# Moving the base inverse of the first two delta heads ahead of the third head's preparation

## The chip, the cores and the metric

The kernel runs on one core of one Trainium2 chip. The metric is the device time of one execution in microseconds (us). The core has five engines that matter here, each with its own queue of instructions, which it works through in order: TensorE (PE for the matmuls, PEld for its weight loads), VectorE (DVE), ScalarE (ACT), GpSimd (POOL), and SyncE (SP), which here issues all DMA transfers.

## The reference

The reference computes one layer of a bidirectional encoder trunk, on 1024 tokens of width 1024, in float32. The layer has three parts, each with a norm before and after it: a mixer, a cross-attention into 256 memory tokens, and a feed-forward network. The change lies in the mixer, which has two branches that start from one input projection: eight heads of windowed attention, and four heads of a gated delta rule, run in both directions. For each delta head, direction and chunk of tokens the delta rule needs the solution of a unit lower triangular system:

```python
lower = jnp.where(strict, jnp.einsum('bhnid,bhnjd->bhnij', kb, k) * decay, 0.0)
tmat = lower + jnp.eye(c, dtype=jnp.float32)
rhs = jnp.concatenate([v * beta[..., None], kb * jnp.exp(g)[..., None]], axis=-1)
sol = lax.linalg.triangular_solve(tmat, rhs, left_side=True, lower=True, unit_diagonal=True)
```

A scan over the chunks follows, which multiplies the solutions with a running state. The outputs of both branches go through one output projection.

## The kernel before

The kernel uses chunks of 128 tokens, eight of them (NT), and inverts each 128 x 128 triangular matrix explicitly, in two steps. The **base inverse** inverts its four 32 x 32 diagonal blocks; the **levels** then join these blocks to 64 x 64 and to 128 x 128 with small matmuls.

The work of the mixer is listed in three tables of short names, ORDER_1 to ORDER_3 (lines 36 to 38), which `issue` (line 700) walks through:

- **D h** (`delta_proj`, line 694) projects key, query and value of delta head h: for each of the three, `proj` (line 264) loads a 512 KB weight tile, splits it into a high and a low part (`split`, line 99: ACT casts, DVE subtracts) and runs 48 matmuls (line 261) into two PSUM banks of the pool `pg`, which has three. `conv` (line 276) then copies the banks with ACT (lines 283, 284) and runs the four other taps of the convolution on DVE (line 286).
- **P h** (`prep`, line 425) makes what the delta rule needs of head h: decays (`gm`, line 457, on DVE, into the matmul of line 458), transposes (line 438), products of keys (line 477) stored to `d_u` (line 480), and the scaled beta values (`beta2`, line 472).
- **B g** (`base_inverse`, line 503) is the base inverse of the pair g of heads (B0 for heads 0 and 1, B1 for heads 2 and 3), all 128 blocks of a pair at once, one in each partition. It transposes `beta2` on PE (line 508), copies it with ACT (line 510), sends it through DRAM (lines 511, 522, 523), loads the blocks from `d_u` into tile `V` (line 515), forms `A` on DVE (lines 525, 527), masks it on POOL (line 528), and then runs 30 rounds of two DVE instructions, each of which needs the one before (lines 534 and 536). Two scalings on DVE (lines 538, 539) and four stores to `d_inv` (line 543) end it. Tiles `V` and `A` exist once, so B1 cannot fill them until B0 has stored them.
- **L h** (`levels`, line 546) fetches the blocks of head h from `d_inv` in 20 small transfers (line 551) and `d_u` (line 572), and joins them: transposes (line 576), then two rounds of a matmul of line 585, a copy on ACT, a matmul of line 591, and copies on ACT and DVE. The result goes to `d_pz` (line 610).
- **G h** and **A ct**, **V** are the projections of the gate and of the attention's queries (A0 to A3), keys (A4) and values. They call the same `proj`. A rotates the result on DVE (lines 726, 727, 732) with four small transfers in between (line 731, tile `rot`), then stores it.
- **W** (`next_windows`, line 678) does two windows of the attention: scores (line 633), softmax, transposes (line 656), products with the values (line 661). Its tiles, among them `vhl` for the values, are in a pool that is opened after the pool of `V` and `A` is closed, so they may lie in the same memory.
- **s01** is a step of the scan of both pairs (`scan`, line 768, matmuls of line 782), **M**, **K**, **V** of ORDER_3 belong to the memory tokens.

```python
ORDER_1 = "D0 P0 D1 P1 D2 P2 D3 P3 B0 B1".split()
ORDER_2 = "L0 L1 G0 G1 A4 V A0 A1 L2 L3 W W W A2 A3 G2 G3 W".split()
ORDER_3 = ("M " + "s01 W K " * 5 + "s01 K " * 3 + "s01 V V").split()
```

The tables do not set the order of the instructions alone. The framework's scheduler (`schedule_with_timeline_sim=True`, line 1512) places every instruction on its engine's queue, by the order in which the code issues it, by what it depends on, and by its own model of durations; loads and splits of weights are raised by a fixed priority (line 120). So instructions of different names come to lie between each other. Once placed, each engine's order is fixed.

Of the kernel before, what the change touches and what calls it, by code (L numbers as in the profile page):

```python
# [32 lines left out]

ORDER_1 = "D0 P0 D1 P1 D2 P2 D3 P3 B0 B1".split()
ORDER_2 = "L0 L1 G0 G1 A4 V A0 A1 L2 L3 W W W A2 A3 G2 G3 W".split()
ORDER_3 = ("M " + "s01 W K " * 5 + "s01 K " * 3 + "s01 V V").split()

# [36 lines left out]
def tile_hybrid_block(  # L76
# [623 lines left out]
    def issue(order, table):  # L700
        for o in order:
            table[o[0]](*(int(c) for c in o[1:]))

    issue(ORDER_1, {"D": delta_proj, "P": lambda h: prep(h, *kqv[h]), "B": base_inverse})
    pp_.close()
# [811 lines left out]
```

## Time and profile before

| what | value |
|---|---|
| median of three runs | 1592.68 us (1585.84 to 1593.12) |
| profiled execution | 1592.72 us, of which 1591.0 us are the span from the first to the last instruction |
| mean granted TensorE clock | 0.976 of full speed |
| busy share of the span: PE, PEld, DVE, ACT, POOL | 96%, 80%, 67%, 44%, 20% |
| matmuls, DVE instructions | 7451, 1774 |
| HBM traffic | 153 GB/s over the span |

All times below are from the profiled execution, in us from the start of its span. How to read the views: "idle before" is the time in which the engine had nothing running just ahead of an instruction, with what ended it behind the arrow; in the table of stages each engine has its busy time and, in brackets, its instructions, then come the granted clock of TensorE (1.00 is full speed), the share of the DMA engines and GB/s; the timeline has the start, the duration, and the instruction. Matmuls are pipelined, so that durations of neighbours overlap: what a matmul takes of PE's time is read from one start to the next. SPq is the queue of SyncE, whose durations are those of issuing a transfer and not of the transfer. L534 is line 534.

### The profile page before, as it was taken

What the parts mean: (1) busy time and instruction counts of PE and PEld (TensorE: products, weight loads), DVE (VectorE), ACT (ScalarE), POOL (GpSimd) and SP (SyncE); (2) the same over time, 40 slices, a digit from 0 to 9 for tenths busy, and PEclk for the clock granted to TensorE, in tenths of its full rate; (3) what the DMA queues carried; (4) which work ended last, traced back from release to release, by engine and by line L of the source; (5) the groups of instructions that cost most, each with busy time, mean ns of one, the idle gap of its engine ahead of it and who ended that gap; (6) DMA issues with size and microseconds to landing.
All of it is one profiled execution on the core that took longest, in us unless ns stands there. A gap on an engine that the chain in (4) does not pass through costs nothing. (4 is left out here: it accounts for less than half of the span.)

```text
span 1591.0 us, 20951 instructions
## 1 busy us (share of the span) xinstructions
PE 1524.5 (96%) x7451; PEld 1270.5 (80%) x7451; DVE 1067.4 (67%) x1774; ACT 706.4 (44%) x1352; POOL 311.2 (20%) x305
## 2 busy tenths in 40 slices
PE   6999999789999998999999999999999999999998
PEld 5888888678899877788888777788888888888776
DVE  6777768766899974443346448776867654587565
ACT  6665551124655563564335565323222332344532
POOL 2000010000002300253302140433434333100021
PEclk9999999886999999999999999999999999999999
DMA  6244354684997484354223164443434333863354
GB/s 205 68 133 129 119 152 132 159 231 116 334 334 258 147 291 151 141 185 155 70 67 108 52 209 149 126 133 118 139 106 153 99 100 100 282 214 113 106 171 160
DMA packets 267366, 247.16 MB, mean 155 GB/s; under 512 B 39016, under 2 KB 204797, under 8 KB 267261
## 3 DMA queue, kind: packets, MB, share of 16 engines
q1 hardware_dynamic: 267261, 245.82, 48.9%
q8 instruction: 59, 0.97, 0.3%
q14 instruction: 46, 0.38, 0.1%
HBM read 173.65 MB, written 69.50 MB: 153 GB/s over the span
## 5 line engine op out<-in xcount | busy, mean ns | idle before, releaser
L102 ACT CAST whi<-wraw 128x1024 fp32r<-128x1024 f32 x108 | 113.2, 1049 | 186.9 <-PE pg L261 37.6
L103 DVE TENSOR_TENSOR wlo<-wraw,whi 128x1024 fp32r<-128x1024 f32 x78 | 95.9, 1231 | 90.5 <-ACT whi L102 86.3
L261 PE MATMUL pg<-hhi,whi 128*128 128x512 f32 x352 | 141.4, 403 | 9.9 <-DVE rop L727 9.9
L261 PE MATMUL pg<-hlo,whi 128*128 128x512 f32 x352 | 140.5, 400 | 0.0
L261 PE MATMUL pg<-hhi,wlo 128*128 128x512 f32 x352 | 139.8, 398 | 0.0
L1013 PE MATMUL pmg<-whi,b 128*128 128x512 f32 x384 | 119.8, 399 | 2.6 <-ACT whi L102 2.2
L1188 PE MATMUL pA<-s,whi 128*128 128x512 f32 x352 | 111.4, 397 | 1.2 <-ACT m L1205 1.2
L103 POOL TENSOR_TENSOR wlo<-wraw,whi 128x1024 fp32r<-128x1024 f32 x30 | 73.8, 2460 | 146.8 <-ACT whi L102 126.3
L261 PEld LDWEIGHTS pg<-hhi,whi 128*128 128x128 f32 x352 | 66.7, 190 | 25.6 <-DVE rop L727 10.0
L1013 PEld LDWEIGHTS pmg<-whi,b 128*128 128x128 f32 x384 | 72.2, 191 | 18.2 <-ACT whi L102 2.6
L261 PEld LDWEIGHTS pg<-hhi,wlo 128*128 128x128 f32 x352 | 66.6, 189 | 15.7
L261 PEld LDWEIGHTS pg<-hlo,whi 128*128 128x128 f32 x352 | 66.6, 189 | 15.2
L1188 PEld LDWEIGHTS pA<-s,whi 128*128 128x128 f32 x352 | 65.2, 187 | 16.8 <-ACT m L1205 1.9
L1378 PE MATMUL pdX<-dhl,whi 128*128 128x512 f32 x264 | 76.0, 390 | 1.9 <-DVE za L1436 1.1
L1013 PE MATMUL pmg<-wlo,b 128*128 128x512 f32 x192 | 71.7, 393 | 0.0
L1188 PE MATMUL pA<-s,wlo 128*128 128x512 f32 x176 | 69.7, 397 | 1.7 <-DVE wlo L103 1.7
L1265 POOL TENSOR_TENSOR act<-act,up 128x512 f32<-128x512 f32 x33 | 50.2, 1521 | 91.5 <-DVE up L1264 54.2
L103 DVE TENSOR_TENSOR wlo<-araw,whi 128x1024 fp32r<-128x1024 f32 (+1 forms) x36 | 40.8, 1133 | 40.2 <-ACT whi L102 40.2
L102 ACT CAST whi<-araw 128x1024 fp32r<-128x1024 f32 (+1 forms) x36 | 35.4, 982 | 71.5 <-PE pdX L1378 24.4
L286 DVE SCALAR_TENSOR_TENSOR acc<-cp,cols,acc 128x1024 f32<-128x1024 f32 x48 | 61.5, 1282 | 1.8 <-ACT acc L284 0.9
L1378 PEld LDWEIGHTS pdX<-dhl,whi 128*128 128x128 f32 x264 | 49.3, 188 | 13.1 <-ACT dhl L102 1.5
L1238 DVE TENSOR_TENSOR sr<-sr,wraw 128x512 f32<-128x512 f32 x22 | 38.1, 1733 | 28.7 <-POOL sr L1237 28.6
(406 smaller groups left out, 4001.8 us busy)
## 6 DMA issues: line engine op xcount, KB each, us to landing
wraw<-in_w_gate_up_dram SPq DMA_DIRECT2D x52, 512.0 KB, 3.9
kv<-d_kv SPq DMA_DIRECT2D x32, 512.0 KB, 6.1
wraw<-in_w_in_dram SPq DMA_DIRECT2D x22, 512.0 KB, 4.5
b<-in_w_down_dram SPq DMA_DIRECT2D x20, 512.0 KB, 6.5
araw<-d_as SPq DMA_DIRECT2D x20, 512.0 KB, 3.7
pz<-d_pz SPq DMA_DIRECT2D x32, 256.0 KB, 5.7
wraw<-in_w_ckv_dram SPq DMA_DIRECT2D x16, 512.0 KB, 6.8
wraw<-in_w_out_dram SPq DMA_DIRECT2D x16, 512.0 KB, 4.1
```

What stands on the lines that cost most here:

```text
L102: nc.scalar.copy(hi, src)
L103: (eng or nc.vector).tensor_tensor(lo, src, f32(hi), ALU.subtract)
L261: nc.tensor.matmul(p_, w[:, k, :], ah[a][:, k, :], start=(k == 0 and i == 0), stop=(k == nk - 1 and i == 2))
L286: nc.vector.scalar_tensor_tensor(acc, cp[:, t:t + S], taps[t], acc, ALU.mult, ALU.add)
L1013: nc.tensor.matmul(pp[t], act[a][:, k, tt], w_[:, kk, :], start=(k == 0 and i == 0), stop=(k == KT - 1 and i == 2))
L1188: nc.tensor.matmul(out_, w[a][:, k, :], xx[b_][:, k, :], start=(start and k == 0 and i == 0), stop=(k == HK - 1 and i == 2), skip_group_ch ...
L1238: nc.vector.tensor_tensor(s[1], s[0], a_[:, 0:HK], ALU.subtract)
L1265: nc.gpsimd.tensor_tensor(o_, o_, up, ALU.mult)
L1378: nc.tensor.matmul(banks[t], a[:, k - k0, tt], w, start=(first and k == 0 and i == 0), stop=(k == NB - 1 and i == 2), skip_group_check=not ...
```

## The change

B0 is moved in ORDER_1 from behind P3 to between D2 and P2. B1 stays where it is, behind P3. Nothing else is changed; the arithmetic is the same, and so is the number of instructions that compute.

```diff
-ORDER_1 = "D0 P0 D1 P1 D2 P2 D3 P3 B0 B1".split()
+ORDER_1 = "D0 P0 D1 P1 D2 B0 P2 D3 P3 B1".split()
```

B0 needs `d_u` of heads 0 and 1 and their part of `beta2`, both of which P1 completes. With the code in the new order the scheduler places all of the mixer's instructions anew.

## The prediction

> **What bounds the kernel now.** I read the page's slices first (40 slices of 39.8 us each), for the stages in which PE is not full or its clock is low.
>
> ```profile
> PE   6999999789999998999999999999999999999998
> DVE  6777768766899974443346448776867654587565
> PEclk9999999886999999999999999999999999999999
> ```
>
> PE is full nearly everywhere, so time can be won only where it isn't: the start, and slices 7 to 9 (280 to 400 us), where the clock is down too. I cut that part into stages at the instructions that bound it.
>
> ```profile
> core 0: us, PE busy (x) PEld busy (x) DVE busy (x) ACT busy (x) POOL busy (x), PEclk, DMA share, GB/s
> 160.70:226.50 65.80, 65.80 (x344) 54.96 (x343) 42.26 (x65) 39.52 (x70) 7.88 (x12) 1.00 0.43 129
> 226.50:280.00 53.50, 53.50 (x240) 43.05 (x239) 47.69 (x97) 10.19 (x14) 1.43 (x2) 1.00 0.50 140
> 280.00:338.80 58.80, 48.91 (x247) 40.95 (x246) 44.92 (x100) 12.66 (x28) 1.43 (x2) 0.88 0.69 185
> 338.80:385.50 46.70, 39.81 (x200) 38.35 (x199) 25.03 (x76) 18.29 (x58) 0.71 (x3) 0.60 0.73 177
> 385.50:409.20 23.70, 19.70 (x85) 16.17 (x83) 15.27 (x44) 13.62 (x38) 2.09 (x5) 0.71 0.48 145
> 409.20:540.00 130.80, 126.90 (x1004) 120.37 (x1005) 125.64 (x348) 72.02 (x204) 23.78 (x33) 1.00 0.87 288
> ```
>
> The first row is P2, D3 and P3; the second B0 beside the gate and attention projections; the third B1 beside the last projections. From 338.80 on no projection is left, and 200 matmuls take 46.7 us at a clock of 0.60. The scan, from 409.2, is full on PE again. In the third stage PE stood still once, in the list of PE's waits from 296 to 415 us:
>
> ```profile
> PE pg L261 <- DVE rop L727: 9.9, 1, 9.9
> ```
>
> Why does the stage from 338.80 have only small matmuls? DVE's timeline gives the ends of B0 and B1 (L539) and the first DVE instruction on the values that the windows need (vhl); PE's gives the places of the levels.
>
> ```profile
> 277.52 1.22 DVE L539 TENSOR_TENSOR A<-A,bB 128x1024 f32<-128x1024 f32 x1
> 286.02 1.22 DVE L527 SCALAR_TENSOR_TENSOR A<-V,b 64x1024 f32<-64x1024 f32 x1 [1.11 <-DMA V<-d_u]
> 334.20 1.22 DVE L539 TENSOR_TENSOR A<-A,bB 128x1024 f32<-128x1024 f32 x1
> 338.90 1.29 DVE L103 TENSOR_TENSOR vhl<-ptv,vhl 128x512 fp32r<-128x512 f32 x2 [2.29 <-ACT vhl L102]
> ```
>
> ```profile
> 298.89 1.87 PE L585 MATMUL ps<-m,L 128*128 128x32 f32 x16
> 300.60 0.48 PE L261 MATMUL pg<-hlo,whi 128*128 128x512 f32 x1
> 313.59 0.80 PE L261 MATMUL pg<-hhi,whi 128*128 128x512 f32 x1 [9.89 <-DVE rop L727]
> 338.81 1.95 PE L591 MATMUL ps<-bs,D 128*128 128x32 f32 x16
> 409.66 0.61 PE L782 MATMUL psc<-kv,pz 128*128 128x128 f32 x4
> ```
>
> B0 ends at 278.7 (277.52 + 1.22), B1 starts 7.3 us later (286.02), since it needs B0's tiles, and ends at 335.4. Levels 0 begin at 298.89; levels 2 and 3 and all windows come after B1's end, when the projections that could fill PE have been used up. So the end of B1 sets when this work may start, and the chain is B0, then B1, then levels and windows, then the scan at 409.66.
>
> **The change part by part.** On DVE, behind the last convolution of D2 (acc), B0's first steps (L525, L527, L534) now stand between those of P2. The difference of DVE's order:
>
> ```order
>  L103 TENSOR_TENSOR wlo<-wraw,whi 128x1024
>  L286 SCALAR_TENSOR_TENSOR acc<-cp,cols,acc 128x1024 x4
> +L525 SCALAR_TENSOR_TENSOR A<-V,bB 64x1024
>  L457 TENSOR_TENSOR gm<-ghi,C 128x512
> +L527 SCALAR_TENSOR_TENSOR A<-V,b_1428 64x1024
>  L457 TENSOR_TENSOR gm<-glo,C 128x512
> ```
>
> The 30 rounds follow, spread over P2, D3 and P3, and end just behind P3. So the change does what it says. PE's order at the end of the projections (pg), before: the levels (m5, L5, D5, L6, D6) and windows (psw) stand alone.
>
> ```order
> L261 MATMUL pg_3744<-hhi1_232,wlo_3740 128x512
> L585 MATMUL ps_2292<-m5_2249,L5_2270 128x32 x4
> L585 MATMUL ps_2299<-m5_2249,L5_2274 128x32 x4
> L591 MATMUL ps_2306<-bs_2297,D5_2120 128x32 x4
> L591 MATMUL ps_2322<-bs_2304,D5_2120 128x32 x4
> L585 MATMUL ps_2338<-mov6_2317,L6_2271 128x64 x4
> L585 MATMUL ps_2345<-mov6_2333,L6_2275 128x64 x4
> L591 MATMUL ps_2352<-bs_2343,D6_2121 128x64 x4
> L591 MATMUL ps_2361<-bs_2350,D6_2121 128x64 x4
> L633 MATMUL psw_3085<-khi_3074,qs_3080 128x256
> ```
>
> And now, one projection earlier in the list:
>
> ```order
> L261 MATMUL pg_3681<-hhi0_146,whi_3677 128x512
> L585 MATMUL ps_2875<-m5_2832,L5_2853 128x32 x4
> L585 MATMUL ps_2882<-m5_2832,L5_2857 128x32 x4
> L633 MATMUL psw_3125<-khi_3074,qs_3120 128x384
> L633 MATMUL psw_3125<-klo_3075,qs_3120 128x384
> L633 MATMUL psw_3130<-khi_3074,qs_3120 128x384
> L633 MATMUL psw_3130<-klo_3075,qs_3120 128x384
> L261 MATMUL pg_3681<-hlo0_147,whi_3677 128x512
> ```
>
> The levels of head 2 (m5_2832) and the second window (psw_3125) have moved in among the matmuls of a projection.
>
> *When does B0 end?* Its DVE work, from the groups of 226 to 340 us, which hold B0 and B1:
>
> ```profile
> L534 DVE TENSOR_TENSOR tmpb<-A 128x30 f32<-128x30 f32 (+14 forms) x60 | 19.9, 331 | 3.2 <-POOL A L528 1.4
> L536 DVE TENSOR_TENSOR A<-A,tmpb 128x30 f32<-128x30 f32 (+14 forms) x60 | 19.8, 331 | 1.5
> L538 DVE TENSOR_TENSOR V<-A,bB 128x1024 f32<-128x1024 f32 x2 | 4.1, 2040 | 0.1
> L525 DVE SCALAR_TENSOR_TENSOR A<-V,bB 64x1024 f32<-64x1024 f32 x2 | 4.1, 2028 | 0.8 <-DMA bB<-d_beta 0.8
> L527 DVE SCALAR_TENSOR_TENSOR A<-V,b 64x1024 f32<-64x1024 f32 x2 | 2.4, 1218 | 1.1 <-DMA V<-d_u 1.1
> L539 DVE TENSOR_TENSOR A<-A,bB 128x1024 f32<-128x1024 f32 x2 | 2.4, 1216 | 0.0
> ```
>
> Half of 19.9 + 19.8 + 4.1 + 4.1 + 2.4 + 2.4 is 26.4 us. In the stage of P2 to P3 DVE has 65.8 - 42.26 = 23.5 us free. If all of it can be used, B0 ends 2.9 us behind it, at 229; if half, 26.4 - 11.8 = 14.6 us behind, at 241. I take 235, 44 us earlier than 278.7. B1 then starts at 242 (the same 7.3 us for stores and loads) and, at its present 49.4 us (286.02 to 335.4), ends at 292. From there to 338.8 there are 47 us in which PE still has projections.
>
> *Term a: the small matmuls move beside projections.* What they are, in the groups of PE from 338.8 to 385.5 us:
>
> ```profile
> L591 PE MATMUL ps<-bs,D 128*128 128x32 f32 (+1 forms) x74 | 14.3, 361 | 0.0
> L585 PE MATMUL ps<-mov,L 128*128 128x64 f32 x32 | 7.3, 415 | 1.8 <-DVE mov L603 1.8
> L633 PE MATMUL psw<-khi,qs 128*128 128x384 f32 (+1 forms) x12 | 6.2, 513 | 3.7 <-DMA qs<-d_q 3.7
> L585 PE MATMUL ps<-m,L 128*128 128x32 f32 x34 | 6.0, 333 | 0.7 <-PE psw L633 0.5 <-DVE L L578 0.2
> L633 PE MATMUL psw<-klo,qs 128*128 128x384 f32 (+1 forms) x12 | 5.5, 456 | 0.0
> L576 PE MATMUL ps<-ident,Ul 128*128 128x128 f32 x16 | 3.5, 392 | 0.0
> L656 PE MATMUL ptw<-ident,sc 128*128 128x128 f32 x16 | 3.0, 352 | 0.7 <-DVE m L635 0.7
> L661 PE MATMUL pow<-ph,vhl 128*128 128x512 f32 x2 | 1.4, 701 | 0.0
> L661 PE MATMUL pow<-pl,vhl 128*128 128x512 f32 x2 | 1.4, 701 | 0.0
> ```
>
> Between projections 16 products of the levels took 1.71 us (298.89 to 300.60), 0.107 each. I price all 74 + 32 + 34 + 16 + 16 = 172 of the levels and transposes so: 18.4 us. The other 28, with up to 512 columns, go at the price of a projection's, 53.5 us for 240 in the second stage, 0.223 each: 6.2 us. Together 24.6 us instead of 46.7: **-22.1 us**. If the 6.9 us of waits in this stage (46.70 - 39.81) come along, it is -15.2. The last 23.7 us before the scan stay as they are: the tail of both PE orders from levels 3 on is nearly the same, and its clock of 0.71 could give at most 0.29 x 23.7 = 6.9 us more.
>
> *Term b: the wait of 9.9 us.* The rotation that it hung on was late because SP first issued the fetches of levels 0 for 20 transfers, here the first, the last and the rotations behind them:
>
> ```profile
> 287.05 0.59 SPq L551 DMA_DIRECT2D m<-d_inv  x1
> 297.20 0.94 SPq L551 DMA_DIRECT2D Z<-d_inv  x2
> 300.15 3.63 SPq L731 DMA_DIRECT2D rot<-sn  x5
> ```
>
> That is 11.1 us (287.05 to 298.14). SP's order now has the same block, of which these are the last rows, ahead of the rotation of the keys (A4):
>
> ```order
> L551 DMA D6_2121<-d_inv00_111 32x8x32
> L551 DMA Z0_2122<-d_inv01_112 32x8x32
> L551 DMA Z1_2123<-d_inv01_112 32x8x32
> L572 DMA Ul_2272<-d_u0_109 128x4x128
> L572 DMA Ul_2276<-d_u0_109 128x4x128
> L731 DMA rot2_2552<-sn_2551 32x512 x4
> ```
>
> Before, this rotation stood ahead of the block. So this collision moves to an earlier projection rather than going away, and the fetches of levels 2 now meet rotations as well. The gain lies between -9.9 and 0; I take half, **-5 us**.
>
> *Term c: P2, D3 and P3 get tighter.* PE runs this stage without a gap, and depends on DVE for gm (L457), at the tightest place of head 3:
>
> ```profile
> 204.13 0.69 DVE L457 TENSOR_TENSOR gm<-ghi,C 128x512 fp32r<-128x512 f32 x1 [1.79 <-PE ps L458]
> 209.29 0.40 PE L458 MATMUL ps<-gm,mL_r 128*128 128x512 f32 x1
> ```
>
> DVE has 209.29 - 204.82 = 4.5 us to spare there. B0's steps overfill the stage by 2.9 us at best, by 14.6 with half of the free time unusable, so PE is late by 0 to 10 us. I take **+2 us**: the overhang may mostly fall behind P3. Hidden are: B0's transpose on PE (one small matmul), its copy on ACT (39.52 busy of 65.8), its mask on POOL (7.88 of 65.8), and on SP its four transfers of beta, now ahead of a gate's weight load, which runs a projection or more ahead of its use; without that cover each would cost its issue, some 0.5 us as above.
>
> The sum is 1592.72 - 22.1 - 5 + 2 = **1567.6 us**, against the profiled execution's own 1592.72, which is the median of 1592.68 within 0.1.
>
> **The rivals.** A measurement of this kernel can tell about 0.5%, 8 us, from no change.
>
> *Two collisions on SP.* The blocks of 20 fetches of B0 and of B1 each hold up a rotation until PE waits as it did, twice 9.9 us: term b becomes -9.9 + 19.8 = +9.9, and the sum 1592.7 - 22.1 + 9.9 + 2 = 1582.5. For it: SP's rows above. Against it: the rotation of A4 has two more PSUM banks' work behind it before PE needs its bank.
>
> *The small products hold up the projections.* PE works in order; a level or window matmul that waits now has projections queued behind it, where it had nothing to lose before. If the levels' chain (matmul, ACT, DVE, matmul) and the windows are late at each place, and the clock falls with it to the 0.60 of the stage that they leave, most of term a goes: the 24.6 us priced at full clock become 24.6 / 0.60 = 41, a is -5.7, b is 0 and c +2: 1589, no change that can be told. Against it: between 298.89 and 300.60 such products ran at full price among projections, and the 0.88 of that stage is what the wait of 9.9 us leaves.
>
> *Only the waits go.* The small products may cost among projections what they cost alone, if the 0.60 is not a matter of their company: a is then the 6.9 us of waits, and the sum 1592.7 - 6.9 - 5 + 2 = 1582.8. Against it: the same 1.71 us for 16 products, where they now take longer (means of 333 to 415 ns in the groups above). The Trainium skill ("TensorE: Matmul & The Clock Gate", section "What's actually happening") has the clock halved by an idle window of about 3.4 us and full again after as long of sustained work. By that rule the 39.81 us of busy PE in 46.70 should already have run at full clock for the most part, and the sum would be the one of this rival; the trace, with 0.60 in that stage, doesn't agree.
>
> *Slower: DVE falls behind in D3 and P3.* If none of the 23.5 us can be used, because DVE's order puts B0's steps where P2's and P3's work is due, gm and the convolutions are 26.4 us late, less 4.5 to spare: PE waits 22 us, and loses clock as in the third stage, where 9.9 us of waiting left 0.88 for 48.9 us of work (5.9 us), so 13 more. B0 then ends near 253 and B1 near 310, which leaves 29 us of projections, enough for two thirds of a at most, -14: 1592.7 + 35 - 14 - 5 = 1609. It decides from 27 us of waiting on, where c eats a and b. Against it: the free time lies in the whole stage, in pieces of 1 to 2 us, and B0's steps are 0.33 us long.
>
> That the scan gives it back can be left out: at 126.90 (PE) and 125.64 (DVE) of 130.80 us it is full, and its rows come in nearly the same order, so it starts earlier and lasts as long.
>
> **How the numbers follow.** The forecast gets 0.64: it rests on PE's order and on prices from rows. Two collisions get 0.14, only the waits 0.03, held-up projections 0.11, slower 0.08. Faster by over 0.5% are the first three, 0.81; the fourth is the same, 0.11; the last slower, 0.08. The range: best is a with the tail's clock and all of b, -22.1 - 6.9 - 9.9 = -38.9, 1553.8; its other end takes in the two rivals near 1582.5. I set 1552 to 1584, which leaves out the two last cases, 0.19.
>
> **What would show it.** Right: L539 of B0 near 235 and of B1 near 292; L633 and levels 2 among L261 rows at a clock of 1.00; the first L782 near 384 instead of 409.66; gaps ahead of L458 or L438 between 160 and 226 of 2 us at most. Wrong: a new wait of L261 on L727, or of L458 on L457, of 10 us and more; B1's end later than 310; or the clock at 0.6 from L633 on while projections still run.

## The result, and the profile after

The changed kernel takes 1566.77 us (median of four, 1565.97 to 1567.66), the one before 1589.31 us over its four runs: ratio 0.9858, 95% interval 0.9826 to 0.9889, so 1.4% faster (22.5 us between the medians). The profiled execution took 1567.12 us with a span of 1565.4, 25.6 us less than before's 1591.0.

The slices of the page, now 39.1 us each, show the dent of slices 7 to 9 nearly filled and the clock at 0.9 or more throughout:

```profile
PE   6999999998999898999999999999999999999998
PEclk9999999999999999999999999999999999999999
```

The same stages as before the change (us, busy time and count of PE, PEld, DVE, ACT, POOL, then clock, DMA share, GB/s):

```profile
160.70:226.50 65.80, 64.48 (x337) 53.83 (x336) 58.61 (x121) 37.94 (x69) 9.65 (x11) 1.00 0.42 129
226.50:280.00 53.50, 51.74 (x253) 43.28 (x252) 45.60 (x94) 13.54 (x26) 2.41 (x2) 0.94 0.67 174
280.00:338.80 58.80, 54.24 (x288) 45.87 (x287) 40.31 (x95) 16.98 (x44) 0.95 (x3) 0.97 0.76 196
338.80:385.50 46.70, 42.00 (x257) 36.51 (x255) 31.52 (x83) 32.20 (x76) 2.34 (x6) 0.93 0.76 242
```

P2 to P3 now carry B0: DVE is busy for 58.61 us instead of 42.26. The stretch from 338.8 on, which had a clock of 0.60, has 0.93. The DVE timeline gives B0's end (first row), B1's start and its end; PE's gives the first levels, the first window, the last projection and the first matmul of the scan:

```profile
231.70 1.22 DVE L539 TENSOR_TENSOR A<-A,bB 128x1024 f32<-128x1024 f32 x1
241.47 2.04 DVE L525 SCALAR_TENSOR_TENSOR A<-V,bB 64x1024 f32<-64x1024 f32 x1 [1.95 <-DMA V<-d_u]
296.39 1.23 DVE L539 TENSOR_TENSOR A<-A,bB 128x1024 f32<-128x1024 f32 x1
```

```profile
253.43 1.87 PE L585 MATMUL ps<-m,L 128*128 128x32 f32 x16
314.12 0.55 PE L633 MATMUL psw<-khi,qs 128*128 128x256 f32 x1 [3.52 <-DMA qs<-d_q]
360.79 0.40 PE L261 MATMUL pg<-hhi,wlo 128*128 128x512 f32 x1
381.67 0.91 PE L782 MATMUL psc<-kv,pz 128*128 128x128 f32 x4
```

B0 ends at 232.9 instead of 278.7, B1 at 297.6 instead of 335.4, and the scan starts 28.0 us earlier (409.66 before). The last projection ends at 361.2 where before it ended at 337.3: it is later, since levels and windows now stand among the projections. What is left behind it, up to the scan, is the row that tells most. Before, then after:

```profile
337.30:409.70 72.40, 61.50 (x298) 56.51 (x298) 40.80 (x120) 33.20 (x97) 2.79 (x8) 0.65 0.65 169
```

```profile
361.20:381.70 20.50, 15.80 (x93) 13.18 (x93) 13.28 (x37) 14.87 (x34) 2.14 (x5) 0.85 0.63 202
```

So 205 matmul records left a stretch that is 51.9 us shorter now, and cost 23.9 us of later projections. Which levels they are, PE's order shows: of the 64 products of L585 on `mov`, 16 for each head, 48 stood in this stretch before, those of heads 1, 2 and 3; 16 stand there now, those of head 3. Head 1's levels need B0 and not B1. PE's waits from 296 to 415 us no longer hold the 9.9 us of L261 on L727:

```profile
PE psw L633 <- DMA qs<-d_q: 3.5, 1, 3.5
...
PE pg L261 <- DVE rop L727: 1.0, 1, 1.0
```

Behind the scan, the rows of L1013 on `b` (their first and last start) tell what of the 28.0 us remains, before and after:

```profile
L1013 PE MATMUL pmg<-whi,b x384: 387/389/632, 642.5 to 933.4; 128*128 128x512 f32 x192
```

```profile
L1013 PE MATMUL pmg<-whi,b x384: 387/389/628, 616.7 to 907.5; 128*128 128x512 f32 x192
```

It is 25.8 us, which stay to the end; 2.2 us were given back in and behind the scan.

### The profile page after: what moved, and what is told of

It is laid out like the page before. It is cut to its first block, busy times and chain, and to the rows that moved or that the text cites. A ratio compares the mean times of both kernels' runs of the same rounds, so it can differ in the third digit from the quotient of the medians.

```text
span 1565.4 us, 20934 instructions
## 1 busy us (share of the span) xinstructions
PE 1507.3 (96%) x7451; PEld 1254.6 (80%) x7451; DVE 1066.1 (68%) x1774; ACT 711.3 (45%) x1356; POOL 311.4 (20%) x305
## 3 DMA queue, kind: packets, MB, share of 16 engines
q1 hardware_dynamic: 267261, 245.82, 49.4%
## 4 chain that ended last, share of the span: by engine, by line
PE 81%; DMA 6%; DVE 6%; issue 2%; ACT 2%; SPq 2%; POOL 0%; DVEq 0%; POOLq 0%; ACTq 0%
PE pg L261 14%; PE pmg L1013 9%; PE pD L1188 8%; PE pE L1188 8%; PE pA L1188 6%; PE pcq L261 6%; PE pdX L1378 6%; PE pdA L1378 4%; PE pB L1188 4%; PE psc L782 3%; PE pdX L1471 2%; PE pdD L1378 2%; PE pcs L1094 1%; PE pco L1120 1%; DMA wraw<-in_w_ckv_dram 1%
## 5 line engine op out<-in xcount | busy, mean ns | idle before, releaser
L261 PE MATMUL pg<-hhi,whi 128*128 128x512 f32 x352 | 142.1, 405 | 1.0 <-DVE rop L727 1.0
L261 PE MATMUL pg<-hhi,wlo 128*128 128x512 f32 x352 | 141.1, 401 | 0.0
L261 PE MATMUL pg<-hlo,whi 128*128 128x512 f32 x352 | 141.0, 401 | 0.0
L1013 PE MATMUL pmg<-whi,b 128*128 128x512 f32 x384 | 119.5, 398 | 2.6 <-ACT whi L102 2.2
L1013 PEld LDWEIGHTS pmg<-whi,b 128*128 128x128 f32 x384 | 71.8, 190 | 18.2 <-ACT whi L102 2.6
L261 PEld LDWEIGHTS pg<-hhi,whi 128*128 128x128 f32 x352 | 67.0, 191 | 16.4 <-DVE rop L727 1.5
L261 PEld LDWEIGHTS pg<-hlo,whi 128*128 128x128 f32 x352 | 67.0, 190 | 14.7
L261 PEld LDWEIGHTS pg<-hhi,wlo 128*128 128x128 f32 x352 | 66.8, 190 | 14.7
L1013 PE MATMUL pmg<-wlo,b 128*128 128x512 f32 x192 | 72.1, 395 | 0.0
```

Of the source, the lines that this page charges most:

```text
L261: nc.tensor.matmul(p_, w[:, k, :], ah[a][:, k, :], start=(k == 0 and i == 0), stop=(k == nk - 1 and i == 2))
L1013: nc.tensor.matmul(pp[t], act[a][:, k, tt], w_[:, kk, :], start=(k == 0 and i == 0), stop=(k == KT - 1 and i == 2))
```

## The experiments

Theory 1 is the prediction's: B1's end sets when levels 2 and 3 and the windows can start, and the gain comes from their running among projections. Ratios are to the kernel before, with 95% intervals. "Stretch" is from the end of the last projection to the first L782. The scheduler places every kernel anew, so a run can change more than its edit says; what else moved is read from its trace.

| kernel | B0's end | B1's end | stretch, us | its clock | ratio |
|---|---|---|---|---|---|
| before | 278.7 | 335.4 | 72.4 | 0.65 | 1 |
| changed | 232.9 | 297.6 | 20.5 | 0.85 | 0.9858 (0.9826 to 0.9889) |
| e1, small matmuls last | 233.1 | 296.2 | 49.0 | 0.76 | 0.9912 (0.9890 to 0.9934) |
| e2, B1 longer | 233.1 | 338.7 | 61.1 | 0.61 | 0.9977 (0.9961 to 0.9992) |
| e3, B0 behind D3 | 254.3 | 326.2 | 54.8 | 0.63 | 0.9961 (0.9947 to 0.9974) |
| e4, B0 behind P1 | 224.2 | 293.1 | 20.0 | 0.91 | 0.9881 (0.9854 to 0.9908) |
| e6, before, no B1 rounds | 277.5 | 294.8 | 53.0 and 17.4 | 0.60 and 0.87 | 0.9994 (0.9982 to 1.0006) |
| e7, before, no B0 rounds | 238.3 | 308.9 | 18.4 | 0.91 | 0.9895 (0.9880 to 0.9910) |

**e1: levels 2 and 3 and the windows behind the last projection.**

```diff
-ORDER_2 = "L0 L1 G0 G1 A4 V A0 A1 L2 L3 W W W A2 A3 G2 G3 W".split()
+ORDER_2 = "L0 L1 G0 G1 A4 V A0 A1 A2 A3 G2 G3 L2 L3 W W W W".split()
```

> The changed kernel with one more edit: levels 2 and 3 and all windows are issued behind the last projection, as the order of before had them, while B0 and B1 stay where the change put them. B1 should end near 297 as now. Theory 1 (the gain comes from small matmuls that run among projections, which B1's end only makes possible): most of term a is lost; with the wait of 9.9 us still gone the time is 1580 to 1590. Theory 2 (the gain comes from the wait that went and from earlier data for levels and windows, wherever these stand): 1575 or less, at most 8 us above the changed kernel.

Measured: 1575.38 us, 0.4 us above theory 2's bound and 4.6 below theory 1's range. Its stretch:

```profile
339.30:388.30 49.00, 42.82 (x238) 38.58 (x235) 35.42 (x104) 29.32 (x84) 2.97 (x8) 0.76 0.65 177
```

The products of heads 2 and 3 and the windows stand alone again, and yet this kernel keeps 0.88% of the changed kernel's 1.42%. Their company of projections is worth the other 0.54%, some 8.6 us. The rest is not free of company: 238 matmuls instead of 298 are left, since head 1's levels, which B0's early end makes possible, still run among projections (32 products of L585 on `mov` are in this stretch, 48 before). PE idles 6.2 us in it instead of 10.9, and the wait of 9.9 us is gone. How these share the 0.88% is not told apart.

**e2: the changed kernel with a longer B1.**

```diff
+            for _ in range(2 * g):
+                nc.vector.tensor_tensor(tv, A[:, j + 1:, j:j + 1].to_broadcast([P, n, j]),
+                                        A[:, j:j + 1, 0:j].to_broadcast([P, n, j]), ALU.mult)
```

> The changed kernel with each multiplication of B1's rounds done three times (60 more instructions on DVE, 19.8 us at 0.33 each; the output is the same). B0's and levels 0's places stay, the end of B1 goes from 297.6 to 320 or later, and the order of PE puts levels 2 and 3 and the windows behind the last projection again. Theory 1 (B1's end sets the time): 1580 to 1590, the gain of the change but for the wait of 9.9 us lost. Theory 2 (B0's early end, its levels and the lost wait carry the gain): within 8 us of the changed kernel, 1575 or less.

Measured: 1585.59 us, as theory 1 has it. B1's last row, and the stretch behind the projections with its longest wait:

```profile
337.42 1.23 DVE L539 TENSOR_TENSOR A<-A,bB 128x1024 f32<-128x1024 f32 x1
```

```profile
338.50:399.60 61.10, 43.33 (x198) 38.32 (x199) 28.06 (x87) 24.23 (x69) 2.68 (x7) 0.61 0.62 163
```

```profile
PE ps L585 <- DMA m<-d_inv: 12.4, 1, 12.4
```

Levels 2 wait 12.4 us for B1's blocks. B0's early end, its levels among projections and the lost wait of L261 together give only 0.23%, 3.7 us, when B1 is late. What e1 has more than this, 0.65%, is B1's earlier end, without company for heads 2 and 3 and the windows.

**e3 and e4: B0 one step later and one step earlier.**

```diff
-ORDER_1 = "D0 P0 D1 P1 D2 B0 P2 D3 P3 B1".split()
+ORDER_1 = "D0 P0 D1 P1 D2 P2 D3 B0 P3 B1".split()   # e3
+ORDER_1 = "D0 P0 D1 P1 B0 D2 P2 D3 P3 B1".split()   # e4
```

> B0 is issued one step later than in the changed kernel, behind D3 instead of D2. It should end near 255, B1 near 317. Theory 1: the order of PE now has all windows and levels 2 and 3 behind the last projection, so little is left of term a, 1578 to 1588. Rival (each microsecond by which B0 ends earlier is worth the same, 25.6 us of gain for 45.8 us): half of the gain, 1578 to 1581; a time near 1567 would say that B0's place doesn't matter as long as it is not behind P3.

Measured: 1582.88 us. B0 ends 24.4 us earlier than before, over half of the change's 45.8, but the gain is a quarter (0.39% of 1.42%). The scan starts at 389.8, 19.9 us earlier, and then loses 11.5 of it: the rows of L1013 on `b` start at 634.1, after a wait of PE that lies between 520 and 640:

```profile
PE pmg L1013 <- ACT b L102: 8.8, 1, 8.8
```

So an early scan is not all of the gain; the work that was pushed behind it comes due later (the last window's scores stand at 603.0, in the changed kernel at 553.8).

> B0 is issued one step earlier than in the changed kernel, behind P1 instead of D2. It should be over long before P3 ends, so that B1 starts as soon as its own input is stored, near 234 instead of 241.5, and ends near 290. Theory 1: some 7 us earlier at the end of B1, with nearly the same order of PE: 1560 to 1567. Rival (DVE's free time in D2 and P2 is too small, and PE waits there for DVE): 1570 or more, with gaps ahead of L458 or L438.

Measured: 1570.23 us, above the 1560 to 1567 of theory 1; its interval overlaps that of the changed kernel. The rival's sign is missing, as PE has no wait between 160 and 226 us, but L261 waits 4.0 us for ACT near 254. B1 ends 4.5 us earlier, which brings nothing: its stretch is 20.0 us.

**e5: before, with the rotations issued by ACT.**

```diff
-                nc.sync.dma_start(rot[32 * q:32 * q + 32], sn[o:o + 32])
+                nc.scalar.dma_start(rot[32 * q:32 * q + 32], sn[o:o + 32])
```

> The kernel before, with the four transfers of each rotation (L731) issued by ACT instead of SP, so that no block of fetches stands ahead of them; B0 and B1 keep their late places. The wait of 9.9 us of L261 on L727 should go. Theory 1 (B1's end sets when levels 2 and 3 and the windows start): the projections end some 10 us earlier, PE then waits for B1 instead, and the time falls by 0 to 4 us, 1585 to 1590. Rival (the wait is worth its own length, as term b counted it at its best): 1578 to 1580.

Measured: 1598.42 us, ratio 1.0055 (1.0038 to 1.0071): slower, which neither had expected. The wait of 9.9 us is gone and the scan starts 8.9 us earlier (400.75), but the scheduler placed the windows later (first scores at 367.64 instead of 353.30, last at 608.05 instead of 577.13), and L1013 on `b` starts at 645.2, 2.7 us later than before. PE now waits 11.0 us, in three pieces, for L603 of the levels. The edit moved too much; what the wait alone costs stays open.

**e6 and e7: before, with the rounds of one pair left out.**

```diff
-        for j in range(1, 31):
+        for j in range(1, 31 if g == 0 else 1):   # e6; e7: g == 1
```

> The kernel before, with the 30 rounds of B1 left out (the inverse of heads 2 and 3 is not computed, 60 instructions of DVE fewer, 19.9 us). B0, levels 0 and 1 and the wait keep their places, B1 should end at 300 to 312 instead of 335.4. Theory 1: levels 2 and 3 and some windows start before the last projection, and the time falls by 14 to 22 us, 1567 to 1575, without any change to B0. Rival (the gain comes from B0, its levels and the wait): 1584 or more.

Measured: 1587.43 us, the same as before. B1 ends even earlier than in the changed kernel, the wait of 9.9 us is gone too, and nothing is won. The stages from the last projection ahead of the levels on:

```profile
280.00:299.40 19.40, 19.38 (x84) 15.18 (x82) 12.15 (x12) 2.64 (x4) 1.42 (x2) 1.00 0.70 166
299.40:352.40 53.00, 44.47 (x216) 42.27 (x217) 29.07 (x85) 20.47 (x61) 0.60 (x3) 0.60 0.67 164
352.40:386.30 33.90, 33.89 (x186) 29.00 (x185) 20.44 (x50) 19.10 (x45) 0.20 (x1) 0.92 0.69 194
386.30:403.70 17.40, 12.01 (x67) 10.11 (x68) 12.48 (x34) 12.43 (x29) 2.14 (x5) 0.87 0.80 268
```

Projections were left, but PE's order has none of them between 299.4 and 352.4: levels of heads 0, 1 and 2 and the first windows stand there in a block of 216 matmuls at a clock of 0.60. B1's early end alone is not enough, and theory 1 as it was stated falls here. What it lacked, as e7 below bears out, is that B0 must be early too, so that its levels are through before B1's are due. That the block comes from both being due together is argued and not shown: the order is the scheduler's, and no other order of this kernel was run.

> The kernel before, with the 30 rounds of B0 left out (the inverse of heads 0 and 1 is not computed, 60 instructions of DVE fewer, 19.9 us), and nothing else changed. B0 should end at 240 to 250 and B1 at 300 to 312. Theory 1: the same gain as without B1's rounds or a little more, since levels 0 and 1 come earlier too: 1565 to 1573. Rival (what helps is DVE's free time in P2 to P3, which only the change uses): 1580 or more.

Measured: 1573.01 us, a gain of 1.05%, with P2 to P3 as they were. DVE's free time there is thus a means to get B0 done, not the source of the gain. It is smaller than theory 1 had it, B1 ending at 308.9.

**e8, e9, e10: large matmuls among the levels' products**, one, or in e9 three, ahead of each group.

```diff
+        def small():
+            t = ps.tile([P, 512], F32, tag="ps", name="ps")
+            nc.tensor.matmul(t, hT[0][0][:, 0, 0:P], hT[0][0][:, 0, :], start=True, stop=True)
+            return t
```

> The kernel before with one more large matmul (128x512, of the first hT slice with itself) ahead of each group of the levels' products, into the same PSUM bank, which the group then overwrites: 40 of them, 9.3 us at the 0.233 each of a projection's rows, output unchanged. Theory 1 (alone the small products are slow because the clock falls without large matmuls among them): the clock of the stretch behind the last projection rises from 0.65 to 0.75 or more, the products get cheaper, and the 9.3 us are paid back at least by half: 1585 to 1594. Rival (the clock there falls for another reason, or the products' price does not hang on it): the clock stays near 0.65 and the time grows by 9 or more, 1598 and up.

> The same with three large matmuls ahead of each group, 120 in all, 28 us at 0.233 each. Theory 1: the clock of that stretch is 0.9 or more, the products of the levels cost there what they cost among projections (means under 300 ns instead of 333 to 415), and the time is well under before plus 28, 1590 to 1605. Rival: 1617 or more.

Measured: 1592.07 us for e8 (1.0023, 1.0009 to 1.0038) and 1599.07 for e9 (1.0060, 1.0043 to 1.0076), by the ratios 3.7 and 9.5 us more for 9.3 and 28 us of added work. The stretch behind the last projection, of e8 and of e9:

```profile
343.20:404.70 61.50, 47.51 (x258) 40.72 (x257) 28.16 (x83) 24.36 (x72) 2.66 (x7) 0.75 0.59 159
```

```profile
354.20:415.30 61.10, 51.28 (x293) 44.98 (x293) 36.21 (x105) 28.14 (x81) 2.84 (x8) 0.90 0.60 161
```

The clock goes from 0.65 to 0.75 and 0.90. One group of products of the levels in that stretch, in before, e8 and e9, of e9 with the fillers ahead of it (busy us, mean ns, idle):

```profile
L585 PE MATMUL ps<-mov,L 128*128 128x64 f32 x48 | 10.6, 406 | 1.8 <-DVE mov L603 1.8
```

```profile
L585 PE MATMUL ps<-mov,L 128*128 128x64 f32 x40 | 7.6, 362 | 2.2 <-DVE mov L603 2.2
```

```profile
L545 PE MATMUL ps<-hhi 128*128 128x512 f32 x60 | 19.4, 437 | 0.0
...
L585 PE MATMUL ps<-mov,L 128*128 128x64 f32 x32 | 4.1, 270 | 0.2 <-DVE mov L603 0.2
```

Useless large matmuls raise the clock of the small products beside them, and these products get shorter: 406 to 362 and 270 ns here, 416 to 339 and 333 in the row of L591 of the same size. So the company of large matmuls does work through the clock. How much of their own cost the fillers pay back is not shown, though the total grew by only 34 to 40% of it: in both runs the wait of 9.9 us of L261 is gone as well, and the scheduler moved some of head 1's products among the projections (40 and 32 are left here of 48).

> The changed kernel with the 40 large matmuls of the first of these runs. Here most products already stand among projections, so there is little to win and the 9.3 us are mostly added. Theory 1: 1570 to 1577. Rival (the fillers help by filling waits, wherever they stand): the same gain or loss against the changed kernel as in the first run against before.

Measured: 1575.47 us (0.9915, 0.9900 to 0.9929), 8.7 us over the changed kernel: where most products have company already, the fillers cost nearly all of their 9.3 us.

**e11 and e12: two tries at a better version.** e11 is the edit of e5 on the changed kernel; e12 gives the rotation's sum to POOL.

> The changed kernel with the transfers of the rotations issued by ACT, the edit that was tried on before. The changed kernel waits only 1.0 us for a rotation, so nothing is to be won; the order of PE puts levels 2 and 3 and the windows some 40 to 60 projection matmuls later, so fewer of them stand among projections. Theory 1: slower than the changed kernel by 3 to 10 us, 1570 to 1577. Rival (the rotations on SP still hold up the projections): 1560 to 1566.

Measured: 1571.18 us (0.9894, 0.9874 to 0.9913). The projections end at 346.6 instead of 361.2, and a stretch of 43.0 us at a clock of 0.68 is left: fewer products in company, as expected. Still it takes no longer than e7 (0.9895), whose stretch is 18.4 us at 0.91, so that stretch is not the whole account.

```diff
-            nc.vector.tensor_tensor(rop, rop, rot, ALU.add)
+            nc.gpsimd.tensor_tensor(rop, rop, rot, ALU.add)
```

> The changed kernel with the sum at the end of each rotation (L732, 0.69 us on DVE) done by POOL, which stands idle most of this part. B1 took 56 us in the changed kernel for 26.4 us of its own DVE work, so DVE is shared there. Theory 1 (an earlier end of B1 is worth something as long as projections are left to mix with): B1 ends 2 to 6 us earlier, levels 2 and 3 follow, and the time falls by 1 to 5 us, 1562 to 1566. Rival (POOL's sum comes later than DVE's did, and the projections wait for their PSUM banks or their keys): 1568 or more, with new waits of L261 or L633.

Measured: 1568.94 us (0.9886, 0.9867 to 0.9906), no different from the changed kernel and above the 1562 to 1566 of theory 1. B1 ends 3.8 us earlier (293.8), but the projections end at 370.7 and the scan starts at 385.1, 3.4 us later than in the changed kernel. The sum takes 1.4 us on POOL where DVE took 0.69; the new waits of L261 or L633 that the rival named are not there. No version tried beats the changed kernel.

## Why the prediction was right, and where its reasons were not

**The sum.** Forecast: -22.1 - 5 + 2 = -25.1 us; the span of the profiled pair fell by 25.6. That it came so near is luck: the terms missed by 2 to 6 us each, and the misses cancelled. The base helped too: 1592.72 is near the top of the four runs before, and between the medians the gain is 22.5 us.

**Ends of B0 and B1.** B0's end at 235 was forecast, 232.9 came. DVE used 58.61 - 42.26 = 16.4 of its 23.5 free us in P2 to P3. For B1, 242 and 292 were forecast, 241.5 and 297.6 came. The step that failed is "at its present 49.4 us": it took 56.1. DVE's busy time in B1's own stretch, before and after, shows why:

```profile
286.02:335.42 49.40, 39.51 (x198) 33.08 (x197) 40.61 (x94) 9.70 (x22) 1.43 (x2) 0.86 0.66 183
```

```profile
241.47:297.62 56.15, 54.39 (x279) 46.08 (x279) 49.58 (x108) 13.67 (x31) 2.42 (x2) 0.94 0.68 181
```

There are 9.0 us more of DVE work in it, with B1's own part the same: work of levels and projections comes between the rounds. It cost little; e4 and e12 ended B1 earlier and won nothing.

**Term a, -22.1.** The stretch behind the projections fell by 51.9 us. The projections' end moved by 23.9, and they waited 8.9 less for L727, so the moved work costs 32.8 there: a is -19.1. Of this some 3.2 are the tail's, which the sum left as it was (see the scan below), so the moved products saved about 16 where 22.1 were forecast. The mis-sized part is the price of a product in company: 32.8 / 205 = 0.160 us with the waits that came along (3.5 us of L633 for `qs` among them), where the prediction had 24.6 / 200 = 0.123.

Its reason was half right. That small products among large ones are cheaper because of the clock is borne out by e8 and e9, and against "only the waits go" stands the measured time, 16 us under that rival's 1582.8. But term a hung all of it on company that B1's end allows, and two things were missing. A third of the level products in the stretch were head 1's, which wait for B0's end and not for B1's. And without company for heads 2 and 3 and the windows 0.88% of 1.42% remain (e1); that data being there in time explains them is argued from e2, where B1 is late and 0.23% remain. e6 shows the other limit: B1's end, named as what "sets when this work may start", is not sufficient. With B0 late, the levels of three heads stand in one block ahead of the last projections, at a clock of 0.60, as low as behind them.

**Term b, -5 of at most -9.9.** It was -8.9. The block of fetches moved to an earlier projection, as forecast, but PE waited 1.0 us there: the rival of two collisions did not happen. How much of the total hangs on this wait alone is not settled (e5). In e2, which doesn't have it either, all that is early but B1 gives 3.7 us, and in e6 the wait is gone without any gain, so the 8.9 us are not a gain by themselves.

**Term c, +2.** Two landmarks of P2 to P3 in the changed kernel:

```profile
209.38 0.40 PE L458 MATMUL ps<-gm,mL_r 128*128 128x512 f32 x1
230.39 0.60 PE L576 MATMUL ps<-ident,Ul 128*128 128x128 f32 x4
```

The first stood at 209.29 before, the second at 229.95: PE is late by 0.1 and 0.4 us. DVE absorbed B0 almost without loss; the rival in which it falls behind needed 27 us of waiting, and the longest wait there is 1.3 us. Nor did products hold up the projections: PE is busy for 54.24 of 58.80 us from 280 to 338.8, at 0.97.

**The scan.** "Starts earlier and lasts as long" was off by 2.2 us. The last 23.7 us ahead of it, which the sum left as they were, are 20.5 now at a clock of 0.85 instead of 0.71, inside the bound of 6.9 us given for it.

## What to carry to other kernels

Small matmuls with a chain through other engines between them are worth placing among large ones: the large ones hold the clock (e8, e9), and they can fill the gaps of the chain. For that the producers must end early, while large matmuls are still left, and, as e6 against e7 suggests, one after the other; where the results were due together, the scheduler set them in a block of their own. How long the stretch without large matmuls is, and its clock, is worth reading beside each engine's busy share, but it does not settle the time (e7 and e11). Work pushed past the next stage has to be looked for as well: the first start of a row well behind it, here L1013 on `b` (642.5 us before, 616.7 changed, 620.7 in e7, 623.7 in e11), followed the time more closely.

## What the runs showed of the hardware

PE loses its clock without one long wait. In e6, PE's timeline at the start of the block and at the return of the projections:

```profile
301.14 1.94 PE L585 MATMUL ps<-m,L 128*128 128x32 f32 x16 [1.76 <-DMA m<-d_inv]
...
352.44 0.77 PE L261 MATMUL pg<-hhi,whi 128*128 128x512 f32 x1
353.02 0.63 PE L261 MATMUL pg<-hlo,whi 128*128 128x512 f32 x1
353.44 0.63 PE L261 MATMUL pg<-hhi,wlo 128*128 128x512 f32 x1
...
361.27 0.40 PE L261 MATMUL pg<-hhi,whi 128*128 128x512 f32 x1
361.50 0.39 PE L261 MATMUL pg<-hlo,whi 128*128 128x512 f32 x1
```

The block's mean clock is 0.60, with 44.47 of 53.0 us busy and no wait over 3.3 us. The projections that follow start 0.58 and 0.42 us apart at first and 0.23 at 361.3, and the granted clock is 0.50 from 352.4 to 357.0 and 0.87 from there to 361.2, so the low clock outlasts the block by some us. The Trainium skill ("TensorE: Matmul & The Clock Gate", section "A second HAM failure mode: psum-queue depth-cycling") describes a kernel whose PE idles briefly between groups of matmuls, so often that its clock is lost and regained. The trace agrees in that the clock is lost here without a long gap. That idle time is the cause the runs do not show: e9, which puts 60 large matmuls into the stretch behind the projections with about the same idle time (9.8 us of 61.1 against 10.9 of 72.4 before), has 0.90 instead of 0.65, and e8, with more of it (14.0 of 61.5), has 0.75. Whether the smallness of the matmuls lowers the clock, their operand type (the kernel has float32 operands in the levels, float32r in the projections and the fillers), or gaps too short to be listed as waits, was not told apart.
